# An eight-tap causal matrix convolution on one core: the first outputs as direct products, and one more block

## The chip, the cores and the metric

The kernel runs on one NeuronCore of one Trainium2 chip. Five engines run their own queues in order and meet only at semaphores: TensorE (PE, matrix multiply into PSUM), VectorE (DVE), ScalarE (ACT), GpSimd (POOL) and SyncE (SP). POOL and SP here mostly issue DMAs: POOL those that also convert fp32 to bf16, SP the stores of the output and the DMA transposes. The metric is the device time in microseconds (us), as a median of runs; lower is better.

## What is computed

`x` has 8 sequences of 4096 steps of 512 features, `kernel` has 8 taps of 512 x 512, and each output is a sum over the eight most recent steps:

```python
for k in range(K):              # K = 8
    shifted = x if k == 0 else concat([zeros(B, k, D), x[:, :-k, :]], axis=1)
    out += matmul(shifted, kernel[k])
```

The steps before a sequence's start count as zero. Inputs and outputs are fp32; the kernel multiplies in bf16 and sums in fp32.

## The kernel before, in words

**Tiling.** All 32768 steps are cut into 128 runs of RUN = 256 steps, one run to a partition. "Row t" is step t of all 128 runs at once, a tile of 128 x 512. Sixteen runs make a sequence, so the seven rows before row 0 are the last seven rows of the run before, moved by one partition, with zeros where a sequence begins. TensorE wants rows with the features on the partitions: `XR` is a ring of R = 20 transposed rows, and row t lies at `place(t) = (t + 4) % 20`.

**Products.** The unit of work is `product` (L116): one transposed row, or a sum of rows, times one 512 x 512 weight, as four matmuls of 128 x 128 by 128 x 512 that accumulate in one PSUM bank. Eight taps done directly would cost eight products per output. The kernel saves most of them by sums. A node (class at L122) computes four outputs with four taps' worth of combined weights. Its kinds are H1 (taps 4 to 7), H0 (taps 0 to 3), PL (their sum) and MI (their difference). Inside a node the four taps are split again in pairs (LO, HI, MID). A node that is not a leaf takes 9 products and a leaf takes 11. Four nodes, PL, MI, H1 and an H0 leaf, give a block of twelve outputs for 38 products, where 96 would be direct.

**What a node does.** `node_z` (L137) sums or subtracts seven rows of the ring into `Z`; `node_s` (L151), `node_A` (L148) and `node_F` (L154) sum those again into the operands; `node_a1`, `node_a0`, `node_u`, `node_v` and `node_l` are products; `node_seed` and `node_dts` are ACT copies between PSUM banks; `node_d` (L200) combines two banks on DVE; `node_e` (L233) takes the result out, and with `middle` (L261) joins it with the other nodes' results and stores it. A node's first product needs `node_A`, its products on `F` need `node_F` and `node_d`.

**Weights.** `load_w` (L266) loads one tap. All other weights are sums of taps, 128 x 2048 elements each: `wsum` (L270) and `plus` (L281) make them on DVE. Four of the PL weights and one of the MI weights are made without DVE: ACT copies or negates a tap (`seed_plus`, or the scalar multiplication at L393), and a DMA issued by POOL adds another tap to it (`add_h0`, L328).

**The head.** The first HEAD = 16 outputs are done in two groups of eight with six nodes: n0 (16 direct products, `direct` at L312, on sums of rows), n1 to n3 (leaves, 11 each) and n4 and n5 (9 each), 67 products in all. Outputs of n0 to n3 wait in SBUF, three of these eight tiles in space that PL weights take later (`held`, L79), until n4 and n5 are added to them by `node_y` (L226), and `store_first` stores them. Rows for the head are loaded into weight tiles not yet in use (`xin`, L287) and transposed on PE (`transpose_pe`, L296) against an identity; `fill` (L293) is two matmuls of zeros whose result nobody uses.

**The order.** The kernel states the order of every queue itself (`manual_schedule`, L49). The head, L331 to L562, is one long list of steps written out. After it NB = 20 blocks of STEP = 12 outputs run through `SLOT` (L563), a list of step names for each kind of node, in which each node's steps are mixed with the preparation of the next two. Loads of `x` go as fp32 to bf16 copies into DRAM (`load_x`) and from there through a DMA transpose on SP (`transpose_x`) into the ring, four rows at a time. PSUM is used as three pairs of banks for outputs and one pair (`pair(3)`) for a node's common terms; a pair is free for its next user when the last reader of its former content is done.

Of the kernel before, what the change touches and what calls it, by code (L numbers as in the profile page):

```python
# [8 lines left out]
LO, HI, MID = 0, 1, 2  # L9
H1, H0, MI, PL = 0, 1, 2, 3  # L10
LEAF = (1, 2, 3)
# [3 lines left out]
def kernel(  # L15
# [13 lines left out]
    HEAD, STEP, R = 2 * K, 12, 20  # L29
# [16 lines left out]
    dpool = ctx.enter_context(tc.tile_pool(name="xd", bufs=NB * STEP // 4, space=bass.MemoryType.DRAM))  # L46
# [6 lines left out]
    W = {}  # L53
# [23 lines left out]
    D4, D42, zero = WP[:, 0:8], Z[:, 0:8], Z[:, 10]  # L77
    E4, T4, T42 = W[MI, MID, HI], W[MI, MID, LO], W[MI, MID, MID]
    held = {(2, 1): WP[:, 8:12], (0, 0): WP[:, 12:16], (0, 1): WP[:, 16:20]}  # L79
# [42 lines left out]
    class Node:  # L122
        def __init__(self, k, t, a, comps=None):
            self.k, self.t, self.a, self.comps = k, t, a, comps
            self.z, self.o = (XR, place(t - 3)) if k < 6 else (Z, 4 if a in (MI, H0) else 0)
            self.leaf = k in LEAF or k >= 6 and a == H0
            self.p = {}
# [31 lines left out]
    def comps(n):  # L159
        s, a = SX[n.k % 2], AX[n.k % 2]  # L160
        u, s = n.comps or (n.z[:, n.o + 3], [s[:, j] for j in range(5)])
        return u, [a[:, 0], a[:, 1]], s, [F[:, j] for j in range(4)]
# [58 lines left out]
    first, cc, dd = {}, {}, {}  # L221
# [4 lines left out]
    def node_y(n, b_, a):  # L226
        y = first[n.t, a, b_]
        tt(y, y, n.p[b_], ADD if a == H1 else SUB)

    def store_first(t, a, b_):  # L230
        store(t + 4 * a + 2 * b_, first[t, a, b_])

    def node_e(n, b_):  # L233
        p, t = n.p[b_], n.t + 2 * b_
        if n.k < 4:
            y = wide(held[n.k, b_]) if (n.k, b_) in held else y_tile()
            nc.scalar.copy(out=y, in_=p)
            first[n.t, n.a, b_] = y
        elif n.k < 6:
            node_y(n, b_, H1)  # L240
            node_y(n, b_, H0)
        elif n.a == PL:
# [42 lines left out]
    H, HF = XR[:, 8:16], wide(WP[:, 0:8])  # L285
    XF = XR[:, 0:8]
    xin = {(0, 0): WP[:, 12:16], (0, 4): WP[:, 16:20], (8, 0): W[PL, LO, LO], (8, 4): W[PL, HI, LO]}  # L287

    def load_xin(t, h):
        rows(xin[t, h], t + h, 4)  # L290

    bank = {}
    def fill(pw):  # L293
        for h in range(2):
            nc.tensor.matmul(pw[:, h], lhsT=zero[:, 0:P], rhs=zero, start=True, stop=True)  # L295
    def transpose_pe(name, k, src, t0, t1):  # L296
        o = pair(k).bitcast(bf).rearrange("p a (b d) -> p (a b) d", b=2)
        for t in range(t0, t1):
            for c in range(DC):
                nc.tensor.transpose(o[:, t - t0, c * P:(c + 1) * P], src[:, t, c * P:(c + 1) * P],  # L300
                                    ident)
        bank[name] = o[:, 0:t1 - t0]
    nodes = [
        Node(0, 0, H1),
        Node(1, 8, H1, (T4[:, 0], [D42[:, 7]] + [T42[:, j] for j in range(4)])),
        Node(2, 0, H0, (D4[:, 4], [D42[:, j] for j in range(3, 8)])),
        Node(3, 8, H0, (D4[:, 4], [D42[:, j] for j in range(3, 8)])),
        Node(4, 0, MI), Node(5, 8, MI)]
    nodes += [Node(6 + 4 * k + i, HEAD + STEP * k, a) for k in range(NB)
              for i, a in enumerate((PL, MI, H1, H0))]  # L310
    n0, n1, n2, n3, n4, n5, n6, n7 = nodes[:8]
    def direct(m, t):  # L312
        n = K // 2 - 1 - m
        product(n0.p[t // 2][:, t % 2], D4[:, t - m] if t >= m else E4[:, 4 + t - m],
                W[H1, n >> 1, n & 1], m == 0)
    def to(z):
        return z.rearrange("p t (c m) -> p t c m", m=P)[:, :, :, 1:P]
    def prev(z):
        return z.rearrange("p t (c m) -> p t c m", m=P)[:, :, :, 0:P - 1]
    def first_run(z):  # L320
        nc.vector.memset(z[:, :, 0:D:G], 0.0)
    X4, X8 = XR[:, 8:12], XR[:, 12:16]
    def start_n0():
        n0.p = {0: pair(0), 1: pair(1)}
    def seed_plus(b_, c_):
        nc.scalar.copy(out=W[PL, b_, c_], in_=W[H1, b_, c_])

# [3 lines left out]
    start_n0()  # L331
    nc.vector.memset(zero, 0.0)
    for k in range(6):
        fill(pair(k % 4))
    load_xin(0, 0)
    fill(pair(2))
    make_identity(nc, ident)
    transpose_pe("x0", 2, xin[0, 0], 0, 2)
    load_xin(0, 4)
    rows(H[:, 1:4], RUN - 7, 3)  # L340
    nc.sync.dma_start(out=HF, in_=xr[:, RUN - 4:RUN, :])
    load_w(4)
    nc.scalar.copy(out=H[:, 4:6], in_=HF[:, 0:2])
    load_w(5)
    nc.scalar.copy(out=H[:, 6:8], in_=HF[:, 2:4])
    nc.scalar.copy(out=XF[:, 4:6], in_=bank["x0"])
    transpose_pe("h0", 3, H, 4, 6)
    nc.scalar.copy(out=to(XF[:, 0:2]), in_=prev(bank["h0"]))
    first_run(XF[:, 0:2])
    fill(pair(3))  # L350
    fill(pair(2))
    tt(D4[:, 0:2], XF[:, 0:2], XF[:, 4:6], ADD)
    transpose_pe("h1", 0, H, 6, 8)
    nc.scalar.copy(out=to(XF[:, 2:4]), in_=prev(bank["h1"]))
    first_run(XF[:, 2:4])
    fill(pair(3))
    fill(pair(3))
    load_xin(8, 0)
    transpose_pe("xb", 0, xin[0, 0], 2, 4)
    direct(0, 0)  # L360
    load_w(6)
    nc.vector.tensor_copy(out=XF[:, 6:8], in_=bank["xb"])
    tt(D4[:, 2:4], XF[:, 2:4], XF[:, 6:8], ADD)
    direct(0, 1)
    transpose_pe("he", 1, H, 1, 4)
    fill(pair(2))
    fill(pair(2))
    seed_plus(HI, HI)
    direct(0, 2)
    transpose_pe("x1", 2, xin[0, 4], 0, 4)  # L370
    tt(to(E4[:, 1:4]), prev(bank["he"]), to(XF[:, 1:4]), ADD)
    first_run(E4[:, 1:4])
    load_w(7)
    fill(pair(3))
    fill(pair(3))
    direct(1, 1)
    nc.vector.tensor_copy(out=X4, in_=bank["x1"])
    fill(pair(3))
    tt(D42[:, 3], D4[:, 1], D4[:, 3], ADD)
    transpose_pe("x2", 2, xin[8, 0], 0, 4)  # L380
    direct(1, 2)
    load_w(3)
    nc.scalar.copy(out=X8[:, 2:4], in_=bank["x2"][:, 2:4])
    tt(D4[:, 4:8], XF[:, 4:8], X4, ADD)
    tt(D42[:, 4:8], D4[:, 2:6], D4[:, 4:8], ADD)
    wsum(H1, MID, HI)
    wsum(H1, MID, LO)
    direct(2, 0)
    nc.scalar.copy(out=X8[:, 0:2], in_=bank["x2"][:, 0:2])
    tt(T4, X4, X8, ADD)  # L390
    direct(0, 3)
    direct(3, 1)
    nc.scalar.mul(out=W[MI, HI, LO], in_=W[H1, HI, LO], mul=-1.0)  # L393
    fill(pair(3))
    direct(3, 0)
    direct(3, 2)
    direct(2, 1)
    wsum(H1, MID, MID)
    tt(AX[1][:, 0], D4[:, 7], T4[:, 0], ADD)
    fill(pair(2))  # L400
    tt(T42[:, 2:4], T4[:, 0:2], T4[:, 2:4], ADD)
    direct(3, 3)
    load_w(1)
    wsum(H0, MID, LO)
    load_w(0)
    load_w(2)
    tt(AX[1][:, 1], T4[:, 0], T4[:, 1], ADD)
    wsum(MI, HI, HI)
    node_a1(n1)
    tt(T42[:, 0:2], D4[:, 6:8], T4[:, 0:2], ADD)  # L410
    direct(2, 2)
    direct(1, 3)
    node_a0(n1)
    node_u(n1)
    node_seed(n1, 0)
    direct(2, 3)
    direct(1, 0)
    wsum(H0, MID, HI)
    wsum(H0, MID, MID)
    load_xin(8, 4)  # L420
    load_x(16)
    node_l(n1, 0, LO)
    tt(AX[0], D4[:, 3:5], D4[:, 4:6], ADD)
    node_e(n0, 0)
    node_seed(n1, 1)
    node_l(n1, 0, HI)
    node_s(n5)
    wsum(MI, LO, HI)
    wsum(MI, MID, HI)
    nc.scalar.copy(out=D4[:, 2:4], in_=T4[:, 2:4])  # L430
    add_h0(MI, HI, LO)
    node_s(n4)
    node_l(n1, 1, HI)
    node_a1(n2)
    wsum(MI, LO, LO)
    node_e(n0, 1)
    node_a0(n2)
    node_e(n1, 0)
    transpose(12, xin[8, 4])
    wsum(MI, LO, MID)  # L440
    tt(D4[:, 4:8], X8, XR[:, 16:20], ADD)
    node_u(n2)
    node_seed(n2, 0)
    seed_plus(LO, HI)
    node_A(n4)
    node_l(n1, 1, LO)
    node_l(n2, 0, LO)
    nc.scalar.copy(out=D42[:, 3], in_=T42[:, 3])
    add_h0(PL, LO, HI)
    node_l(n2, 0, HI)  # L450
    node_seed(n2, 1)
    node_a1(n3)
    node_l(n2, 1, LO)
    tt(AX[1], D4[:, 3:5], D4[:, 4:6], ADD)
    node_u(n3)
    node_a0(n3)
    wsum(MI, MID, LO)
    behind(AX[1][:, 0])
    load_x(36)
    node_e(n1, 1)  # L460
    node_l(n2, 1, HI)
    node_e(n2, 0)
    node_seed(n3, 1)
    node_seed(n3, 0)
    wsum(MI, MID, MID)
    node_a1(n4)
    transpose_x(16)
    tt(D42[:, 4:8], D4[:, 2:6], D4[:, 4:8], ADD)
    node_l(n3, 0, LO)
    node_F(n4, 1)  # L470
    node_l(n3, 0, HI)
    plus((MID, LO))
    node_e(n2, 1)
    plus((MID, HI))
    node_e(n3, 0)
    load_x(20)
# [160 lines left out]
```

## Time and profile before

| what | value |
|---|---|
| median of three runs | 758.33 us (757.30 to 759.14) |
| the profiled execution | 759.11 us, its span 757.3 us |
| PE, DVE, ACT, POOL busy in the span | 733.1, 690.1, 254.9, 62.0 us |
| weight loads on PE from `product` | 3308 (827 products of four) |
| first matmul of a `product` begins | 15.61 us |
| last PE work in the chain of waits ends | 752.8 us |

"Busy" for PE includes fills and transposes. Matmul records can be missing, so products are counted by the weight loads, of which none is. In the page's slices PE is busy to nine tenths or more from the seventh slice of 18.9 us on, up to the last one, and falls below that in slices 1, 5 and 6. DVE is busy to nine tenths from the sixth slice on, up to the last.

### The profile page before, as it was taken

What the parts mean: (1) busy time and instruction counts of PE and PEld (TensorE: products, weight loads), DVE (VectorE), ACT (ScalarE), POOL (GpSimd) and SP (SyncE); (2) the same over time, 40 slices, a digit from 0 to 9 for tenths busy, and PEclk for the clock granted to TensorE, in tenths of its full rate; (3) what the DMA queues carried; (4) which work ended last, traced back from release to release, by engine and by line L of the source; (5) the groups of instructions that cost most, each with busy time, mean ns of one, the idle gap of its engine ahead of it and who ended that gap; (6) DMA issues with size and microseconds to landing.
All of it is one profiled execution on the core that took longest, in us unless ns stands there. A gap on an engine that the chain in (4) does not pass through costs nothing.

```text
span 757.3 us, 8900 instructions
## 1 busy us (share of the span) xinstructions
PE 733.1 (97%) x3352; PEld 331.8 (44%) x3420; DVE 690.1 (91%) x727; ACT 254.9 (34%) x380; POOL 62.0 (8%) x103
## 2 busy tenths in 40 slices
PE   6999689999999999999999999999999999999997
PEld 2544234444444444444444444444444444444443
DVE  1774899999999999999999999999999999999996
ACT  4264332333333233333323333332423323232331
POOL 5020201010010101101010110101011010100000
PEclk9999899999999999999999999999999999999999
DMA  9979797976959688796968869796786969775424
GB/s 206 207 140 162 195 255 173 211 200 161 245 136 237 162 195 215 149 238 148 243 160 180 241 140 236 146 238 168 185 234 136 242 145 224 184 178 169 136 84 167
DMA packets 159948, 141.51 MB, mean 187 GB/s; under 512 B 130208, under 2 KB 134304, under 8 KB 159776
## 3 DMA queue, kind: packets, MB, share of 16 engines
q1 hardware_dynamic: 145456, 99.89, 48.6%
q0 software_dynamic: 14304, 40.77, 29.6%
q8 instruction: 27, 0.44, 0.2%
q10 hardware_dynamic: 144, 0.26, 0.1%
q14 instruction: 17, 0.14, 0.1%
HBM read 77.33 MB, written 98.57 MB: 232 GB/s over the span
## 4 chain that ended last, share of the span: by engine, by line
PE 91%; DMA 4%; DVE 2%; issue 1%; ACT 0%; POOL 0%; DVEq 0%; ACTq 0%; POOLq 0%
PE pp L118 91%; DMA w<-in_kernel_dram 2%; DMA out_dram<-w 1%; DMA XR<-xd 1%; DVE y L82 1%; DVE w L82 1%; PE pp L295 0%; DVE S L82 0%; PE pp L300 0%; ACT pp L188 0%; DVE Z L82 0%; DVE F L82 0%; ACT pp L169 0%; ACT pp L190 0%; DVE pp L82 0%
## 5 line engine op out<-in xcount | busy, mean ns | idle before, releaser
L118 PE MATMUL pp<-w,S 128*128 128x512 bf16 x1114 | 261.6, 381 | 5.7 <-ACT pp L190 3.9
L118 PE MATMUL pp<-w,F 128*128 128x512 bf16 x973 | 245.3, 379 | 2.9 <-DVE pp L82 1.7
L118 PE MATMUL pp<-w,A 128*128 128x512 bf16 x668 | 173.2, 380 | 3.1 <-ACT pp L169 0.7
L118 PEld LDWEIGHTS <-S 128*128 128x128 bf16 x1136 | 111.2, 98 | 140.7 <-issue 9.5
L82 DVE TENSOR_TENSOR Z<-XR 128x3584 bf16<-128x3584 bf16 (+2 forms) x104 | 146.9, 1430 | 4.1 <-DMA XR<-xd 4.1
L118 PEld LDWEIGHTS <-F 128*128 128x128 bf16 x992 | 97.0, 98 | 119.5 <-issue 2.3
L82 DVE TENSOR_TENSOR S<-Z 128x2560 bf16<-128x2560 bf16 x80 | 118.4, 1480 | 0.0
L188 ACT COPY pp<-pp 128x1024 f32<-128x1024 f32 (+1 forms) x85 | 58.7, 691 | 157.5 <-PE pp L118 152.7
L118 PEld LDWEIGHTS <-A 128*128 128x128 bf16 x680 | 66.2, 98 | 85.7 <-issue 5.2
L172 ACT COPY pp<-pp 128x512 f32<-128x512 f32 x62 | 35.3, 570 | 201.2 <-PE pp L118 201.2
L118 PE MATMUL pp<-w,Z 128*128 128x512 bf16 x378 | 96.8, 379 | 1.0 <-DVE w L82 0.5
L82 DVE TENSOR_TENSOR F<-S 128x1024 bf16<-128x1024 bf16 x124 | 84.5, 682 | 0.0
L107 POOL COPY junk<-A 128x2 bf16<-128x2 bf16 x19 | 18.6, 978 | 540.3 <-DVE A L82 540.3
L190 ACT ACTIVATE pp<-pp 128x1024 f32<-128x1024 f32 (+1 forms) x85 | 59.6, 701 | 4.8 <-DVE y L82 3.8
L118 PEld LDWEIGHTS <-Z 128*128 128x128 bf16 x388 | 38.0, 98 | 46.4 <-issue 0.8
L207 DVE SCALAR_TENSOR_TENSOR pp<-pp,DT 128x512 f32<-128x512 f32 x62 | 42.9, 692 | 16.3 <-PE pp L118 15.6
L247 DVE SCALAR_TENSOR_TENSOR y<-pp,y 128x1024 f32<-128x1024 f32 x40 | 48.8, 1220 | 8.6 <-PE pp L118 8.1
L82 DVE TENSOR_TENSOR A<-Z 128x1024 bf16<-128x1024 bf16 x80 | 54.9, 686 | 1.3
L82 DVE TENSOR_TENSOR y<-y,pp 128x1024 f32<-128x1024 f32 (+1 forms) x46 | 54.3, 1187 | 1.9 <-PE pp L118 1.9
L244 ACT ACTIVATE y<-pp 128x1024 f32<-128x1024 f32 x40 | 41.1, 1027 | 42.2 <-PE pp L118 42.2
L82 DVE TENSOR_TENSOR y<-pp,y 128x1024 f32<-128x1024 f32 x40 | 48.6, 1216 | 1.7 <-DMA out_dram<-y 1.7
L262 DVE SCALAR_TENSOR_TENSOR y<-y 128x1024 f32<-128x1024 f32 x40 | 48.6, 1216 | 0.0
(53 smaller groups left out, 278.8 us busy)
## 6 DMA issues: line engine op xcount, KB each, us to landing
out_dram<-y SPq DMA_DIRECT2D x124, 512.0 KB, 7.7
xd<-in_x_dram POOLq DMA_DIRECT2D x60, 512.0 KB, 10.8
w<-in_kernel_dram POOLq DMA_DIRECT2D x8, 512.0 KB, 20.8
w<-w POOLq DMA_DIRECT2D x5, 512.0 KB, 6.8
w<-in_x_dram POOLq DMA_DIRECT2D x4, 512.0 KB, 11.7
out_dram<-w SPq DMA_DIRECT2D x3, 512.0 KB, 6.8
w<-in_x_dram SPq DMA_DIRECT2D x1, 1024.0 KB, 4.9
XR<-xd SPq DMA_TRANSPOSE x60, 5.4
```

The source lines that it names most:

```text
L82: nc.vector.tensor_tensor(out=o, in0=a, in1=b, op=op)
L107: nc.gpsimd.tensor_copy(out=junk, in_=z[:, 0:2])
L118: nc.tensor.matmul(bank, lhsT=comp[:, c * P:(c + 1) * P], rhs=w[:, c, :], start=start and c == 0, stop=c == DC - 1, skip_group_check=True)
L172: nc.scalar.copy(out=n.q[:, 0], in_=n.q[:, 1])
L188: nc.scalar.copy(out=o, in_=q)
L190: nc.scalar.mul(out=o, in_=q, mul=-1.0)
L207: nc.vector.scalar_tensor_tensor(out=p[:, 0], in0=p[:, 1], scalar=-1.0, in1=DT, op0=MUL, op1=SUB)
L244: nc.scalar.mul(out=cc[b_], in_=p, mul=0.5)
L247: nc.vector.scalar_tensor_tensor(out=dd[b_], in0=p, scalar=-0.5, in1=cc[b_], op0=MUL, op1=ADD)
L262: nc.vector.scalar_tensor_tensor(out=cc[b_], in0=cc[b_], scalar=2.0, in1=dd[b_], op0=MUL, op1=SUB)
```

## The change

The head's node tree goes. The first HEAD = 4 outputs are 4 x 8 direct products of a row and a tap (`direct(tap, t)`), and NB = 21 blocks follow from t = 4, all of PL, MI, H1 and H0 (leaf). The class loses what only the head's nodes used; `node_y`, `store_first`, `first`, `held`, the tiles D4, D42, E4, T4 and T42, and every call of `add_h0` and `seed_plus` go. All combined weights come from `wsum` and `plus` on DVE. The rows 0 to 3 are loaded by SP as fp32 into `XF` and cast by DVE and ACT; rows 4 to 7 and 8 to 11 come by POOL, the last ones in two loads of two rows. The steps of the first four nodes are also written out one by one, through `go(k, name)`, which runs the step of that name as `SLOT` would. In that list a call that has nothing to do (such as `go(3, "v1")`, whose next node is a leaf) emits nothing.

```diff
-LEAF = (1, 2, 3)
+LEAF = ()
...
-    HEAD, STEP, R = 2 * K, 12, 20
+    HEAD, STEP, R = K // 2, 12, 20
...
-    D4, D42, zero = WP[:, 0:8], Z[:, 0:8], Z[:, 10]
-    E4, T4, T42 = W[MI, MID, HI], W[MI, MID, LO], W[MI, MID, MID]
-    held = {(2, 1): WP[:, 8:12], (0, 0): WP[:, 12:16], (0, 1): WP[:, 16:20]}
+    H, zero = WP[:, 0:8], DT.bitcast(bf)[:, 0:D]
+    xin = {0: W[MI, MID, MID], 4: W[MI, MID, HI], 8: W[MI, MID, LO]}
...
-    def node_y(n, b_, a):
-        y = first[n.t, a, b_]
-        tt(y, y, n.p[b_], ADD if a == H1 else SUB)
...
+    def history(eng, t, name):
+        z = XR[:, place(t):place(t) + bank[name].shape[1]]
+        eng(out=to(z), in_=prev(bank[name]))
         nc.vector.memset(z[:, :, 0:D:G], 0.0)
+    def here(eng, t, name, a, b):
+        eng(out=XR[:, place(t) + a:place(t) + b], in_=bank[name][:, a:b])
+    def cast(eng, a, b):
+        eng(out=xin[0][:, a:b], in_=XF[:, a:b])
+    def direct(tap, t):
+        n = K - 1 - tap
+        product(pd[t // 2][:, t % 2], XR[:, place(t - tap)], W[n >> 2, n >> 1 & 1, n & 1], tap == 0)
+    def direct_out(b_):
+        y = y_tile()
+        nc.scalar.copy(out=y, in_=pd[b_])
+        store(2 * b_, y)
+    def z_rows(n, a, b):
+        zsum(a, n.t - 3 + a, n.t + 1 + a, b - a, ADD)
+    def s_rows(n, a, b):
+        tt(SX[n.k % 2][:, a:b], Z[:, a:b], Z[:, a + 2:b + 2], ADD)
...
+    pd = {0: pair(0), 1: pair(1)}
+    load_w(0)
+    rows(H[:, 4:8], RUN - 4, 4)
+    make_identity(nc, ident)
+    nc.vector.memset(zero, 0.0)
+    nc.sync.dma_start(out=XF, in_=xr[:, 0:4, :])
+    cast(nc.vector.tensor_copy, 2, 4)
+    for k in range(7):
+        fill(pair(2 + k % 2))
+    cast(nc.scalar.copy, 0, 2)
+    transpose_pe("x0", 2, xin[0], 0, 4)
+    load_w(4)
+    here(nc.scalar.copy, 0, "x0", 2, 4)
+    load_w(5)
+    load_w(1)
+    here(nc.scalar.copy, 0, "x0", 0, 2)
+    load_w(7)
+    direct(0, 3)
+    direct(0, 2)
+    transpose_pe("h4", 3, H, 4, 8)
+    history(nc.scalar.copy, -4, "h4")
+    load_w(3)
+    plus((HI, HI))
+    wsum(H1, HI, MID)
...
+    load_w(6)
+    direct(1, 0)
+    rows(H[:, 1:4], RUN - 7, 3)
...
+    load_w(2)
+    load_xin(4)
...
+    load_xin(8, 0, 2)
...
+    transpose_pe("x8", 2, xin[8], 0, 2)
+    here(nc.scalar.copy, 4, "x4", 0, 2)
+    here(nc.scalar.copy, 4, "x4", 2, 4)
+    fill(pair(3))
+    transpose_pe("x9", 2, xin[8], 2, 4)
+    direct(7, 1)
+    direct(6, 1)
+    wsum(MI, LO, HI)
+    direct(5, 0)
+    wsum(PL, LO, MID)
+    direct(6, 0)
+    load_x(12)
+    here(nc.scalar.copy, 8, "x8", 0, 2)
+    wsum(MI, MID, HI)
+    wsum(PL, MID, MID)
+    wsum(MI, LO, MID)
+    z_rows(nodes[1], 0, 5)
+    load_x(16)
+    node_A(nodes[1])
+    here(nc.scalar.copy, 10, "x9", 0, 2)
+    z_rows(nodes[1], 5, 7)
+    direct_out(0)
+    node_a1(nodes[1])
+    load_x(20)
+    load_x(24)
+    s_rows(nodes[1], 0, 3)
+    direct(2, 3)
+    node_u(nodes[1])
...
+    s_rows(nodes[1], 3, 5)
+    transpose_x(12)
+    node_z(nodes[2])
+    node_A(nodes[2])
+    node_F(nodes[1], 0)
...
+    for k in range(5, len(nodes)):
+        for name in SLOT[nodes[k].a].split():
+            go(k, name)
```

## The prediction

> **What bounds the kernel now.** I first split the span into stages by windows, for the instructions of `product` alone. Columns: stage, its length, PE busy (records), weight loads busy (records), granted clock, DMA share, GB/s. Four weight loads are one product.
>
> ```profile
> 0.00:15.50 15.50, 0.00 (x0) 0.00 (x0) 1.00 0.95 205
> 15.50:46.00 30.50, 24.59 (x101) 10.49 (x105) 0.94 1.16 202
> 46.00:77.00 31.00, 29.58 (x134) 13.27 (x136) 1.00 0.75 136
> 77.00:103.40 26.40, 18.06 (x66) 7.11 (x67) 0.87 0.90 218
> 103.40:757.30 653.90, 646.16 (x2940) 292.58 (x3000) 1.00 0.76 187
> ```
>
> From 103.4 to 430 us the trace has 1510 weight loads in 326.6 us: 216.3 ns each, **0.865 us a product**, with no room between them. So from 103.4 us on PE is the bound, and nothing there can be gained except by fewer products. Before that, 77 products (308 loads) are worth 66.6 us and take 103.4. **Lost: 36.8 us**, by stage: 15.5 with no product, then 30.5 - 26.25 x 0.865 = 7.8 (row transposes, fills, clock), 31.0 - 34 x 0.865 = 1.6, and 26.4 - 16.75 x 0.865 = 11.9. After the last product 4.4 us pass to the end of the span.
>
> Next, what made the fourth stage lose 11.9 us, by the timeline (start, duration, instruction, in brackets the idle time before it and who ended it):
>
> ```profile
> 75.43 1.23 DVE L82 TENSOR_TENSOR Z<-XR 128x2048 bf16<-128x2048 bf16 x1 [4.06 <-DMA XR<-xd]
> 81.77 3.57 PE L118 MATMUL pp<-w,S 128*128 128x512 bf16 x8 [3.86 <-ACT pp L190]
> 91.44 1.23 DVE L82 TENSOR_TENSOR w<-w,w 128x2048 bf16<-128x2048 bf16 x1 [1.99 <-DMA out_dram<-w]
> 99.70 1.02 PE L118 MATMUL pp<-w,F 128*128 128x512 bf16 x3 [1.72 <-DVE pp L82]
> ```
>
> DVE waits for transposed rows, then runs behind: PE waits for an ACT seed that itself waited for `node_y` on DVE. Eight matmuls then start 446 ns apart. At 91 us a weight sum waits until an output held in weight space is stored. DVE is busy 24.4 of these 26.4 us (all-engine windows).
>
> **The price of the change in PE work.** Before, 67 + 20 x 38 = 827 products; after, 32 + 21 x 38 = 830: **+2.6 us**. Transposes stay 76, fills go from 18 to 13. The tail keeps its steps, 4.4 us. All else is how much is lost in the new head, so I lay it out queue by queue.
>
> **Loads (POOL).** Its timeline before:
>
> ```profile
> 8.41 0.74 POOL L88 DMA_DIRECT2D w<-in_kernel_dram  x1 [1.29 <-DMA w<-in_x_dram]
> 10.85 0.74 POOL L88 DMA_DIRECT2D w<-in_kernel_dram  x1 [1.70 <-DMA w<-in_x_dram]
> 12.71 0.74 POOL L88 DMA_DIRECT2D w<-in_kernel_dram  x1 [1.12 <-DMA XR<-in_x_dram]
> 15.75 0.74 POOL L88 DMA_DIRECT2D w<-in_kernel_dram  x1 [2.30 <-DMA w<-in_kernel_dram]
> 18.25 0.54 POOL L88 DMA_DIRECT2D w<-in_x_dram  x1 [1.76 <-DMA w<-in_kernel_dram]
> 20.71 0.56 POOL L88 DMA_DIRECT2D xd<-in_x_dram  x1 [1.92 <-DMA w<-in_x_dram]
> ```
>
> The ninth to fourteenth load each wait for the landing of the first to sixth, in order of issue. So these starts are landings: 2.4 us for four rows, 1.9 for three, 3.0 and 2.5 for a weight, 2.5 for four rows. I take 2.65 a weight and 0.63 a row; this puts the last weight of before at 36.7, and DVE's wait for a weight indeed ends at 36.79. **A rule speaks against the change here**: the Trainium skill (DMA: Bandwidth & Descriptors, "Anatomy of one DMA") has a DMA cost about 2.0 us fixed plus bytes over 436 GB/s, so smaller parts pay the fixed part again. A weight (1.05 MB) would be 4.4 us and halving the load of rows 8 to 11 would add 2.0. The row says 2.5 to 3.0 and 1.9 for the smaller piece: with eight loads in flight the fixed part lies under the others. I take the row. The rule, read as a serial price, is the third rival.
>
> The first load lands near 8.4 again (the SP load of 1 MB runs beside it, as before). Then, in the new order: rows -4..-1 at 10.9, tap 4 at 13.6, tap 5 16.2, tap 1 18.9, tap 7 21.5, tap 3 24.2, tap 6 26.8, rows -7..-5 28.7, tap 2 31.3, rows 4..7 33.8, rows 8,9 35.1, rows 10,11 36.3, rows 12.. 38.8. The last weight comes 5.4 us earlier than before because two tiles of rows moved behind it. None of these issues waits for an engine.
>
> **PE in the head.** Fills from 1.2 to 7.2 (fourteen at 427 ns, the spacing of the first ones before). Rows 0..3 land at 5.7 (SP load before); the casts take 1.0 on ACT (`CAST` row) and between 0.69 (DVE COPY of 1024) and 1.04 on DVE, both under the fills: nothing. Sixteen transposes 1.1, ACT copy 1.0: first product at **9.5 instead of 15.6**. Then I follow the listed order with 0.865 a product against the landings. `history` of four rows is not in the trace: 1.0 (half of it) to 2.0 (two halves); I take 1.9, and `direct(4, 3)` starts at 14.9. `direct(4, 1)` ends 18.8, `(1, 0)` waits for tap 1 until 18.9; `(7, 3)` ends 24.9, `(3, 0)` 28.3, the second history's transposes 30.9, `(2, 2)` 32.6, `(7, 0)` 37.1. The transposes of rows 10,11 use the PSUM pair of rows 8,9, so PE waits for that copy, 38.1 to 38.8, and behind it stand the last four products. They end at **42.9**; 31 products are done, 16.1 us lost. No gap exceeds 1 us.
>
> **DVE in the head.** Sums run back to back at 1.13 us start to start:
>
> ```profile
> 26.72 2.35 DVE L82 TENSOR_TENSOR w<-w,w 128x2048 bf16<-128x2048 bf16 x2
> L82 DVE TENSOR_TENSOR S<-Z 128x2560 bf16<-128x2560 bf16 x80 | 118.4, 1480 | 0.0
> L82 DVE TENSOR_TENSOR Z<-XR 128x3584 bf16<-128x3584 bf16 x36 | 72.5, 2014 | 0.0
> ```
>
> There were 21 on DVE, now 26: +5.7 us, while five ACT copies of 1.9 and five accumulating DMAs go. Starting at 15.0 (tap 4, then behind the history's memset), the first 22 end at 40.5. They wait for a landing only at taps 5 and 1. Rows 8,9 are copied by 38.8, so `z_rows(0, 5)` runs to 41.9, `node_A` to 42.5, `z_rows(5, 7)` to 43.1, the two parts of `s` to 44.6. Splitting costs little: 1.40 + 0.60 against 1.93 start to start for z, nothing that matters for s. What it buys is that `node_A` need not wait for rows 10,11 (copied 40.5), 0.6 us. With `A` at 42.5, PE goes straight on at 43.3 after a fill: no stall at the first node.
>
> **The first block.** Both engines, step by step: PE finishes node 1's `v1` at 48.5, `a1` of node 2 at 49.4 (its `A` 47.1), `l00` 50.2 (its `d` 48.3), `a0` 52.0 (weight sum MID, LO done 50.6), `u` 52.8 (51.8), `v0` 55.4 (S at 53.2), `a1` of node 3 57.1 (A at 56.3), `v1` of node 3 63.1. Then `a1` of node 4 waits for the last sum (MID, MID) until **64.1**: 1.0 stall. At 64.1, 54 products are done: 64.1 - 46.7 = **17.4 lost**. DVE has hardly a gap from 15 to 78 us here, against 96.6% in the steady stage (315.4 of 326.6), where it has about 1.1 us a block free. So whatever DVE is late, PE loses once, and it isn't soon made up.
>
> **What I can't walk.** Rows 16 to 27 come by transposes that SP issues behind the two stores of the direct outputs and when the ring's old rows are read: about 56 and 63 us, needed by `node_z` of node 5 at 70.8. With 5.4 us a transpose (DMA issues) and 512 KB stores ahead (7.7), that is close; the second block's `z` is queued on DVE ahead of everything that PE needs next. The bounds are 0 and 11.9, the loss of the corresponding stage before; I take **3.5**, near the 4.06 that DVE waited for rows there, as the second block has three sets of rows to come but few stores. The node additions (eight of 1.2 us), the held outputs and the adding DMAs, which made the rest of the 11.9, are gone.
>
> **The clock.** The Trainium skill (TensorE: Matmul & The Clock Gate, "The HAM clock gate") halves the clock after an idle window of some 3.4 us. In the trace 1.64 us idle before 15.61 sufficed for matmuls 427 ns apart until 18.9; 0.73 at 46.67 didn't. By the rule a 1.5 us stall in the first block is free, by the row it can add 1.7 (eight matmuls at 0.21). I count it within the 3.5.
>
> **The sum.** Loss 17.4 + 3.5 = 20.9 for 36.8, a gain of 15.9, less 2.6: **-13.3**. On the profiled execution: 757.3 - 13.3 = 744.0 of span, 745.8 with the 1.8 outside it (759.11). The median was 0.8 below this execution: **745.0**. With the unwalked term at its bounds: 741.5 to 753.4.
>
> **Rivals.**
> *A, the wait moves (747 to 756.8).* DVE has no slack: if weights land 3 us later, or each of some 60 operations takes 0.1 more, DVE is 5 to 6 us later at the first block; PE loses that and a cold stretch of 1.7, beside rows as late as before: 753. For it: 100% DVE and the wait at 75.43. Against it: sums overlap at 1.13 as observed.
> *B, as walked with nothing unwalked: 741.5.* For it: PE had no stall in any later block of before, and few stores run early.
> *C, loads bound the head: slower.* All the direct products and 22 sums need taps in the order of one queue. By the rule's serial price each weight is 1.75 and each four rows 1.9 later than by the row (three rows as much), so tap 2 lands 7 x 1.75 + 2 x 1.9 = 16.1 later, and rows 10,11, behind three more loads, about 22. The first node starts 16 to 22 later, and it turns slower from 13.3; at 18 the time is 763. Against it: six landings in the trace.
> *D, within 0.2%:* only if A's two losses and half of C's come together.
>
> **Chances.** Forecast (742 to 747, B's end included) 0.53, A 0.30, D 0.05, C 0.12. A measurement tells 0.2% (1.5 us) from no change. Faster 0.83, same 0.05, slower 0.12. The range, 740 to 757, leaves out C, D and a little below.
>
> **What would show it.** First product at 9.5; last direct product but one near 43; fewer than 22 us lost in the first 103 us; no PE idle over 2 us. A PE gap at 24 to 35 ended by a weight's landing speaks for C; DVE waiting for `XR<-xd` near 70, or PE for DVE between 60 and 90, for A. The forecast is wrong if the landings exceed 2.65 us or the steady stage has idle PE.

## The result, and the profile after

746.34 us (746.14 to 746.51, four runs) against 757.82 us for the kernel before in the same comparison: a ratio of 0.985, 95% interval 0.983 to 0.9865. The forecast was 745.0, with a range of 740 to 757. The span of the profiled execution went from 757.3 to 744.8 us. Over all comparisons, executions of the kernel before took 754.7 to 759.5 us, so the profiled one, at 759.1, lies near the top of its spread, and what profiles differ by is somewhat more than what medians differ by.

The windows of the kernel after, for `product` alone (L117 there; stage, length, PE busy, weight loads, clock, DMA share, GB/s):

```profile
0.00:15.50 15.50, 3.76 (x16) 1.56 (x18) 1.00 0.97 197
15.50:46.00 30.50, 25.72 (x113) 11.05 (x115) 1.00 1.15 211
46.00:77.00 31.00, 28.23 (x128) 12.57 (x130) 1.00 0.72 165
77.00:103.40 26.40, 25.58 (x117) 11.53 (x118) 1.00 0.91 211
103.40:744.80 641.40, 633.49 (x2884) 286.86 (x2940) 1.00 0.76 185
```

At 216.3 ns each, the 381 weight loads up to 103.4 us are worth 82.4 us: **21.0 lost, where it was 36.8**. By stage: 11.6 (15.5), 5.6 (7.8), 2.9 (1.6), 0.9 (11.9). The fourth stage gave 11.0 us and the start 3.9; twelve more weight loads cost 2.6. After 103.4 us, 5.5 us aren't products, against 5.0. Sum: 15.8 - 2.6 - 0.5 = 12.7; the spans differ by 12.5.

How the head runs, by PE's timeline (start, duration, instruction, idle time before it and who ended it):

```profile
9.48 1.90 PE L117 MATMUL pp<-w,XR 128*128 128x512 bf16 x8
40.07 0.61 PE L280 MATMUL pp<-ident,w 128*128 128x128 bf16 x8 [0.67 <-ACT XR L296]
44.40 1.03 PE L117 MATMUL pp<-w,A 128*128 128x512 bf16 x4
48.38 1.02 PE L117 MATMUL pp<-w,A 128*128 128x512 bf16 x4 [1.21 <-ACT pp L189]
55.31 1.02 PE L117 MATMUL pp<-w,Z 128*128 128x512 bf16 x4 [0.72 <-ACT DT L193]
63.91 1.02 PE L117 MATMUL pp<-w,Z 128*128 128x512 bf16 x4 [0.68 <-ACT DT L193]
82.05 1.02 PE L117 MATMUL pp<-w,A 128*128 128x512 bf16 x4 [0.70 <-ACT pp L187]
```

The first product begins at 9.48 us. Node 1 begins at 44.40 without a wait, and the four short waits from there to 82 us are all for ScalarE copies, none for VectorE or a DMA. `a0` of nodes 1 and 5 stands behind seed copies in the list, and `u` of nodes 2 and 3 behind a copy into `DT`, on the same pair of banks.

POOL's timeline, where the waits again end at landings (first to sixth, tenth and twelfth load):

```profile
9.40 0.55 POOL L87 DMA_DIRECT2D w<-in_x_dram  x1 [1.26 <-DMA w<-in_kernel_dram]
11.86 0.74 POOL L87 DMA_DIRECT2D w<-in_kernel_dram  x1 [1.91 <-DMA w<-in_x_dram]
14.45 0.54 POOL L87 DMA_DIRECT2D w<-in_x_dram  x1 [1.84 <-DMA w<-in_kernel_dram]
16.95 0.54 POOL L87 DMA_DIRECT2D w<-in_x_dram  x1 [1.96 <-DMA w<-in_kernel_dram]
19.49 0.53 POOL L87 DMA_DIRECT2D w<-in_x_dram  x1 [2.00 <-DMA w<-in_kernel_dram]
23.07 0.55 POOL L87 DMA_DIRECT2D xd<-in_x_dram  x1 [3.04 <-DMA w<-in_kernel_dram]
32.53 0.52 POOL L87 DMA_DIRECT2D xd<-in_x_dram  x1 [2.02 <-DMA w<-in_kernel_dram]
36.25 0.52 POOL L87 DMA_DIRECT2D xd<-in_x_dram  x1 [0.69 <-DMA w<-in_x_dram]
```

VectorE in the same time, by windows of all engines (busy time of PE, PEld, DVE, ACT, POOL):

```profile
15.50:43.00 27.50, 25.82 (x149) 12.85 (x151) 26.47 (x24) 5.38 (x5) 4.74 (x9) 1.00 1.16 210
43.00:65.00 22.00, 19.33 (x89) 8.47 (x88) 21.03 (x24) 9.50 (x14) 0.00 (x0) 1.00 0.99 213
65.00:80.00 15.00, 14.89 (x69) 6.84 (x70) 14.96 (x16) 4.15 (x6) 1.72 (x4) 1.00 0.40 94
```

VectorE is busy 96% from 15.5 to 43, 96% to 65 and 99.7% to 80 us. PE loses 2.7 of the 22 us in the middle and nearly nothing from 65 on. ScalarE, in contrast, is busy for only 5.4 of the 27.5 us up to 43.

### The profile page after: what moved, and what is told of

It is laid out like the page before. It is cut to its first block, busy times and chain, and to the rows that moved or that the text cites. A ratio compares the mean times of both kernels' runs of the same rounds, so it can differ in the third digit from the quotient of the medians.

```text
span 744.8 us, 8881 instructions
## 1 busy us (share of the span) xinstructions
PE 729.3 (98%) x3354; PEld 331.0 (44%) x3422; DVE 697.2 (94%) x729; ACT 241.3 (32%) x369; POOL 57.8 (8%) x98
## 4 chain that ended last, share of the span: by engine, by line
PE 93%; ACT 1%; issue 1%; DVE 1%; DVEq 0%; ACTq 0%
PE pp L117 92%; ACT pp L187 0%; DVE w L81 0%; PE pp L280 0%; ACT DT L193 0%; ACT XR L296 0%; DVE pp L81 0%; DVE pp L206 0%; DVE y L81 0%; ACT pp L189 0%; DVEq L625 0%; ACT pp L168 0%; ACT pp L171 0%; PE pp L274 0%; DVE F L81 0%
## 5 line engine op out<-in xcount | busy, mean ns | idle before, releaser
L117 PE MATMUL pp<-w,S 128*128 128x512 bf16 x1153 | 269.0, 379 | 1.5
L117 PE MATMUL pp<-w,F 128*128 128x512 bf16 x986 | 248.4, 379 | 1.0
L117 PEld LDWEIGHTS <-S 128*128 128x128 bf16 x1176 | 114.8, 98 | 140.2 <-issue 3.6
L117 PE MATMUL pp<-w,A 128*128 128x512 bf16 x659 | 170.5, 379 | 2.7 <-ACT pp L189 1.2
L81 DVE TENSOR_TENSOR Z<-XR 128x2048 bf16<-128x2048 bf16 (+3 forms) x109 | 154.6, 1437 | 0.1
L117 PEld LDWEIGHTS <-F 128*128 128x128 bf16 x1008 | 98.6, 98 | 119.0
L81 DVE TENSOR_TENSOR S<-Z 128x2560 bf16<-128x2560 bf16 (+1 forms) x85 | 124.8, 1469 | 0.0
L187 ACT COPY pp<-pp 128x512 f32<-128x512 f32 x84 | 57.3, 682 | 158.8 <-PE pp L117 154.0
L117 PEld LDWEIGHTS <-A 128*128 128x128 bf16 x672 | 65.2, 97 | 82.8 <-DVE A L81 4.5
L171 ACT COPY pp<-pp 128x512 f32<-128x512 f32 x63 | 35.9, 570 | 198.9 <-PE pp L117 198.9
L117 PE MATMUL pp<-w,Z 128*128 128x512 bf16 x330 | 85.4, 379 | 1.7 <-ACT DT L193 1.4
L189 ACT ACTIVATE pp<-pp 128x512 f32<-128x512 f32 x84 | 58.1, 692 | 1.1 <-PE pp L117 1.1
L206 DVE SCALAR_TENSOR_TENSOR pp<-pp,DT 128x512 f32<-128x512 f32 x63 | 43.9, 697 | 14.5 <-PE pp L117 14.5
L81 DVE TENSOR_TENSOR y<-y,pp 128x1024 f32<-128x1024 f32 (+1 forms) x43 | 51.1, 1190 | 2.0 <-PE pp L117 1.9
L117 PEld LDWEIGHTS <-Z 128*128 128x128 bf16 x336 | 32.9, 98 | 41.4 <-issue 1.5
## 6 DMA issues: line engine op xcount, KB each, us to landing
xd<-in_x_dram POOLq DMA_DIRECT2D x61, 512.0 KB, 10.8
w<-in_kernel_dram POOLq DMA_DIRECT2D x8, 512.0 KB, 15.9
```

Source lines behind the costliest of these rows:

```text
L81: nc.vector.tensor_tensor(out=o, in0=a, in1=b, op=op)
L117: nc.tensor.matmul(bank, lhsT=comp[:, c * P:(c + 1) * P], rhs=w[:, c, :], start=start and c == 0, stop=c == DC - 1, skip_group_check=True)
L171: nc.scalar.copy(out=n.q[:, 0], in_=n.q[:, 1])
L187: nc.scalar.copy(out=o, in_=q)
L189: nc.scalar.mul(out=o, in_=q, mul=-1.0)
L206: nc.vector.scalar_tensor_tensor(out=p[:, 0], in0=p[:, 1], scalar=-1.0, in1=DT, op0=MUL, op1=SUB)
```

## The experiments

Two theories went into them. **T:** in the head and the first block PE follows the landing of the taps, then VectorE's queue; what VectorE is late, PE loses once. **R:** the waits for ScalarE seen above set the first block, and VectorE is only busy. For the kernel before: VectorE's queue lost the 11.9 us (T), or late rows and stores did (R).

The runs were made on several chips; the kernel before ran beside each of them (medians of 756.5 to 758.1 us), the kernel after again only beside the three runs on GpSimd sums, halved weights and the order of rows.

**The kernel after, once more,** beside those three:

> The kernel after, unchanged, beside the next three on the same chip. All theories: 746.3 us (746.1 to 746.5 so far), with single executions up to 1.5 us later where the first weight lands later or the clock rises later.

Measured: 746.45 us (746.04 to 747.33). One of its four runs is 0.8 above the rest.

**More work on VectorE.**

```diff
     wsum(MI, LO, MID)
+    for _ in range(3):
+        wsum(PL, LO, MID)
     z_rows(nodes[1], 0, 5)
```

> The kernel after, with one weight sum (PL; LO, MID) made three times more on VectorE just ahead of the first node's row sums: 3 x 1.13 = 3.4 us more work in VectorE's queue. Theory (VectorE has no slack in the head, and PE waits for it once): the whole delay reaches the end, 746.3 + 3.4 = 749.7 us, the first product of node 1 moves from 44.4 to about 47.3 us, and the product losses before 103 us grow by about as much. Rival (the waits for ScalarE's copies, not VectorE, set the first block): VectorE's delay is half absorbed, under 748 us. Rival (VectorE catches up within some blocks, and PE with it): nothing, 746.3.

Measured: 752.2 us (751.79 to 752.88), 5.8 more, for 3.4 us of work. Its PE timeline, at node 1's first product, and the window with the clock:

```profile
48.18 1.89 PE L117 MATMUL pp<-w,A 128*128 128x512 bf16 x4 [3.26 <-DVE A L81]
```

```profile
44.10:65.00 20.90, 15.70 (x64) 6.49 (x63) 18.44 (x20) 8.34 (x12) 0.00 (x0) 0.92 0.77 164
```

PE waits 3.26 us for `A`, and four matmuls then take 1.89 us in place of 1.03: the clock falls to 0.92 on average over 20.9 us, 1.7 us worth. Node 1 begins 3.8 us later than in the kernel after (48.18 for 44.40), and the cold stretch adds its 1.7, which makes up the difference of the spans (750.3 and 744.8). So the delay comes through whole, and the gap that it opens costs half as much again. Later nothing is caught up. T, and more than T said.

**Fewer waits for ScalarE.**

```diff
-    node_seed(nodes[1], 0)
-    node_seed(nodes[1], 1)
     node_a0(nodes[1])
+    node_seed(nodes[1], 0)
+    node_seed(nodes[1], 1)
     node_dts(nodes[1])
...
-    go(1, "dt")
     go(1, "u")
+    go(1, "dt")
```

(likewise for node 3; node 5's `a0` moves up behind its `u`).

> The kernel after, in which node 1's a0 product stands before the two seed copies, and the DT copies of nodes 2 and 3 stand behind the u product; node 5's a0 moves behind its u. Theory (four waits of PE for ScalarE in the first block, 1.21, 0.72, 0.68 and 0.70 us, come from the order of a copy and a product on the same pair of banks): three to four of these waits vanish, 746.3 - 2.5 = about 743.8 us. Rival (VectorE, busy without a gap, is what sets the block): PE waits for VectorE's row and weight sums instead, and the time stays within 0.7 us of 746.3.

Measured: 746.29 us (745.98 to 747.88): no gain in the median. The four waits did go, but shorter ones for VectorE (0.19 twice) and others for ScalarE (0.71 and 0.30 up to node 4) came in their place. The chain of waits of that kernel runs through VectorE from 51.9 to 68.6 us with pauses of at most 0.38; its last pieces, and PE's timeline:

```profile
63.82 1.39 DVE S L81
65.21 1.14 DVE y L232
66.35 1.13 DVE Z L81
67.48 1.15 DVE w L81
68.62 0.04 issue
68.67 14.85 PE pp L117 x68
```

```profile
10.56 3.07 PE L117 MATMUL pp<-w,XR 128*128 128x512 bf16 x8 [1.83 <-DMA w<-in_kernel_dram]
50.80 1.89 PE L117 MATMUL pp<-w,S 128*128 128x512 bf16 x8 [0.71 <-ACT pp L187]
60.94 1.04 PE L117 MATMUL pp<-w,A 128*128 128x512 bf16 x4 [0.19 <-DVE A L81]
68.67 1.02 PE L117 MATMUL pp<-w,Z 128*128 128x512 bf16 x4 [0.19 <-DVE w L81]
```

(This profiled execution began its direct products 1.1 us late and cold, and its node 1 at 46.46, 2.1 us behind the one above.) In the kernel after, VectorE ended the last weight sum at 67.06 and PE took it up at 67.37: the two were level within 0.3 us.

```profile
50.37 0.69 DVE L81 TENSOR_TENSOR pp<-DT,pp 128x512 f32<-128x512 f32 x1 [0.80 <-PE pp L117]
65.84 1.22 DVE L81 TENSOR_TENSOR w<-w,w 128x2048 bf16<-128x2048 bf16 x1
67.37 1.03 PE L117 MATMUL pp<-w,Z 128*128 128x512 bf16 x4
```

So R fails in the main: most of the waits for ScalarE were worth nothing by themselves. Not quite all: from node 1 to node 4 PE took 22.97 us in the kernel after and 22.21 here, 0.76 of the 2.6 us of waits. The median shows none of it; as the kernel after did not run on that chip, the worth is only known to lie between nothing and about 0.8.

**Rows not divided.**

```diff
-    load_xin(8, 0, 2)
+    load_xin(8)
...
-    load_xin(8, 2, 4)
...
-    z_rows(nodes[1], 0, 5)
+    z_rows(nodes[1], 0, 7)
```

(transposes, copies and `s_rows` undivided in the same way).

> The kernel after, with rows 8 to 11 loaded, transposed, copied and summed undivided (one load of four rows, one copy of 2048, one row sum of seven rows, one of five). By the prediction's working, node 1's A waits for rows 10 and 11 and for a sum of seven rows instead of five: about 0.6 us on VectorE and up to 1.5 on PE, where the wait of 0.67 us for the pair of banks goes away: 746.5 to 748. By the rule that each load pays about 2.0 us anew, the undivided form saves it: 744.5 to 745.5.

Measured: 748.37 us (748.0 to 748.67): dividing is worth about 1.9 us, somewhat more than the working had. PE's timeline:

```profile
45.21 1.04 PE L117 MATMUL pp<-w,A 128*128 128x512 bf16 x4 [0.97 <-DVE A L81]
```

Node 1 now waits 0.97 us for VectorE and begins 0.8 later than in the kernel after. The rest isn't placed: the profiled execution's first weight landed 1.0 us later than the other's, though its last one did not. The smaller loads in any case cost nothing.

**Smaller loads everywhere.**

```diff
-        load(W[n >> 2, n >> 1 & 1, n & 1], kr[:, :, tap, :])
+        for c in (0, 2):
+            load(W[n >> 2, n >> 1 & 1, n & 1][:, c:c + 2], kr[:, c:c + 2, tap, :])
```

> The kernel after, with each of the eight weights loaded by two DMAs of half the size. By the landings in the trace (pace set by bytes, the fixed part hidden by the loads in flight): the landings stay within 1 us and the time within 1 us of 746.3. By the rule of about 2.0 us fixed for each DMA, paid one after the other: the last weight lands 8 x 2.0 = 16 us later and the time is near 746.3 + 14 = 760.

Measured: 745.86 us (745.5 to 746.25), 0.6 less than the kernel after beside it, though the two ranges overlap. POOL's timeline:

```profile
12.47 0.71 POOL L87 DMA_DIRECT2D w<-in_kernel_dram  x1 [0.61 <-DMA w<-in_kernel_dram]
13.71 0.71 POOL L87 DMA_DIRECT2D w<-in_kernel_dram  x1 [0.53 <-DMA w<-in_kernel_dram]
14.99 0.71 POOL L87 DMA_DIRECT2D w<-in_kernel_dram  x1 [0.57 <-DMA w<-in_kernel_dram]
```

A half takes 1.24 to 1.28 us from landing to landing, half of a whole one. The fixed 2.0 us that the Trainium skill gives a DMA (DMA: Bandwidth & Descriptors, "Anatomy of one DMA") is not paid in series with eight in flight. What part of a load's latency it makes, these runs don't show: a half took a median of 10.3 us from issue to landing, a whole one 15.9.

**Rows ahead of the last weights.**

```diff
+    load_xin(4)
+    load_xin(8, 0, 2)
+    load_xin(8, 2, 4)
     load_w(6)
```

(and gone from behind them).

> The kernel after, with rows 4 to 11 loaded before taps 6 and 2 instead of behind them (as the kernel before had two tiles of rows ahead of its last weights). Taps 6 and 2 land 8 x 0.63 = 5.0 us later. Theory (PE and VectorE follow the landing of the taps): the sums and products that need taps 6 and 2 wait, the head ends 3 to 5 us later, with a cold stretch of up to 1.7 us: 749.5 to 753. Rival (VectorE's 22 sums, not the landings, set the head): under 1.5 us, below 748.

Measured: 751.18 us (749.95 to 751.64), 4.7 more. PE's timeline at the first product of tap 6:

```profile
32.67 3.33 PE L117 MATMUL pp<-w,XR 128*128 128x512 bf16 x8 [3.82 <-DMA w<-in_kernel_dram]
```

A wait of 3.82 us for the tap, then eight matmuls in 3.33 us. The order of the loads is worth this much.

**No first fills.** The line `fill(pair(2 + k % 2))` and its loop go.

> The kernel after, without its first seven fills (fourteen matmuls of zeros up to 7.2 us). By the trace of before (matmuls 427 ns apart for some 3.3 us after an idle time) the transposes and the first products run cold: 8 to 12 matmuls at 0.21 us more, so PE is 1.7 to 2.5 us later until 15 us, where it waits for the history in any case; part is absorbed there: 747 to 748.5. If the clock doesn't matter here: 746.4 or less.

Measured: 747.5 us (747.15 to 748.1), 1.1 more. PE's timeline:

```profile
6.56 1.89 PE L280 MATMUL pp<-ident,w 128*128 128x128 bf16 x16 [6.56 <-ACT w L304]
8.24 2.13 PE L274 MATMUL pp<-DT 128*128 128x512 bf16 x4
10.58 2.72 PE L117 MATMUL pp<-w,XR 128*128 128x512 bf16 x8 [0.21 <-DMA w<-in_kernel_dram]
```

Sixteen transposes take 1.89 us for 1.05, and eight matmuls 2.72 for 1.90. So the fills keep the clock up, and without them 0.8 us are lost twice. But how much of the 1.1 this makes is not shown: the first weight of this execution also landed 1.4 us later (at 10.8 for 9.4), and the first of the two losses lies ahead of that landing.

**The kernel before, part by part.** First without its node additions:

```diff
     def node_y(n, b_, a):
-        y = first[n.t, a, b_]
-        tt(y, y, n.p[b_], ADD if a == H1 else SUB)
+        pass
```

> The kernel before, with the additions of nodes 4 and 5 to the held outputs left out (eight VectorE additions of 1.2 us; the outputs 0 to 15 lack that part). Theory (VectorE's queue is what loses 11.9 us from 77 to 103 us): about 8 x 1.13 = 9 us come off VectorE's queue there and the loss shrinks by 6 to 9 us: 749 to 752 us. Rival (transposed rows and the stores that hold weight space set that stage): the loss shrinks by less than 3 us, 755 us or more.

Measured: 754.82 us (751.78 to 756.0) against 758.0: 3.2 less, between the two theories. From 77 to 103.4 us its profile has 92 weight loads, a loss of 6.5 us for 11.9. Its chain of waits shows what is next, and PE's timeline the wait at its end:

```profile
80.70 1.91 ACT w L325
82.61 0.28 issue
82.90 4.39 DMA w<-w
87.29 0.04 issue
87.33 1.04 PE pp L118 x4
```

```profile
87.33 1.02 PE L118 MATMUL pp<-w,Z 128*128 128x512 bf16 x4 [1.99 <-DVE w L82]
```

A sum made by a ScalarE copy (1.91 us) and an adding DMA (4.39): work taken off VectorE, but a chain of 6.6 us on the path. So I took it away too, with the sums on VectorE where the DMA stood:

```diff
-    seed_plus(HI, HI)
...
-    add_h0(PL, HI, HI)
+    plus((HI, HI))
```

(likewise for the other four).

> The kernel before, with the node additions left out as in the earlier run of it (the outputs 0 to 15 lack the part of nodes 4 and 5), and with its five sums by ScalarE copy and adding DMA made on VectorE at the place of the DMA. Theory (what is left of the loss from 77 to 103 us is the chain copy 1.9 us, adding DMA 4.4 us, next sum): five sums of 1.13 us join VectorE's queue, the chain goes, and the loss of that stage falls from 6.5 to under 4 us: 750 to 752.5, against 754.8 with the chain. Rival (VectorE's queue alone): 5.7 us more on VectorE, 757 or more.

Measured: 750.76 us (750.67 to 751.93) against 757.71. Its window for `product`, and VectorE's row sums that had waited for transposed rows:

```profile
77.00:103.40 26.40, 24.56 (x112) 10.72 (x111) 1.00 0.83 179
```

```profile
69.07 2.09 DVE L82 TENSOR_TENSOR Z<-XR 128x1536 bf16<-128x1536 bf16 x2
```

2.4 us lost. So of the 11.9 us some 5.4 went with the additions, 4.1 with the copies and adding DMAs, though VectorE got five more sums, and 2.4 stay. That is by the profiles; by the medians the additions are worth 3.2 and both together 7.0 us. Part of the difference is clock: in this stage it was 0.87 before (3.4 us worth), 0.94 without the additions and 1.00 here. VectorE's wait for transposed rows, 4.06 us before, was still 3.96 without the additions; here it is gone. So it came with the copies and adding DMAs.

**Two sums on GpSimd.**

```diff
-    wsum(H0, MID, HI)
-    wsum(H0, MID, MID)
+    pool_sub(W[H0, MID, HI], W[H0, HI, HI], W[H0, LO, HI])
+    pool_sub(W[H0, MID, MID], W[H0, MID, LO], W[H0, MID, HI])
```

(`pool_sub` is a subtraction on GpSimd, behind `load_x(32)`.)

> The kernel after, with the two weight sums that the first block needs last (H0; MID, HI and MID, MID) made by GpSimd from about 37 us on instead of VectorE: 2 x 1.13 = 2.3 us less in VectorE's queue between 59 and 67 us. Theory (VectorE and the waits for ScalarE's copies are level at the fourth node, within 0.3 us): the waits for the copies still stand, so 0.3 to 0.8 us are gained, 745.5 to 746. Rival (VectorE alone is the bound): 2.3 us gained, 744. Rival (GpSimd's sum and VectorE's operations slow each other, or GpSimd's sums take over 15 us each): same or slower, 746.3 to 749.

Measured: 757.33 us (756.4 to 758.01), 10.9 more. The timelines of POOL and VectorE:

```profile
35.02 9.08 POOL L271 TENSOR_TENSOR w<-w,w 128x2048 bf16<-128x2048 bf16 x2
34.75 5.43 DVE L81 TENSOR_TENSOR w<-w 128x2048 bf16<-128x2048 bf16 x1
40.10 5.08 DVE L81 TENSOR_TENSOR w<-w,w 128x2048 bf16<-128x2048 bf16 x1
```

Two VectorE sums of 1.2 us took 5.4 and 5.1 while GpSimd made its two. VectorE lost about 8 us just ahead of node 1; PE waited 7.69 us there and lost clock as well. Node 1 began 7.5 us later than in the kernel after, and node 4 another 1.7. No theory had it so dear.

**VectorE and ScalarE relieved together.** The first try put four edits together: products ahead of the copies, weights in halves, and two sums made by copy and adding DMA.

```diff
+    seed_minus(LO, HI)
...
+    nc.scalar.mul(out=W[H0, MID, HI], in_=W[H0, LO, HI], mul=-1.0)
...
     load_x(12)
+    add_h0(MI, LO, HI)
+    nc.gpsimd.dma_start(out=W[H0, MID, HI], in_=W[H0, HI, HI], accum_op=ADD)
```

> The kernel after with four edits together: the products ahead of the ScalarE copies as in the earlier run, the weights in halves, and two weight sums taken off VectorE (MI; LO, HI and H0; MID, HI) by a negating ScalarE copy in its idle time before 37 us and an adding DMA behind the load of rows 12 to 15. Theory (VectorE's queue and PE's waits for ScalarE are level, so only both together bring something): 2 x 1.13 + 0.3 from the block and 0.5 from the first landing, 743.2 to 744.3. Rival (the adding DMAs delay the rows or the sums behind them): 745.5 or more.

Measured: 749.54 us (748.65 to 749.81), 3.1 worse than after. VectorE's timeline:

```profile
42.39 1.23 DVE L81 TENSOR_TENSOR w<-w,w 128x2048 bf16<-128x2048 bf16 x1 [4.43 <-DMA w<-w]
```

I had overlooked that the sum MI; MID, HI, ahead of node 1 in VectorE's queue, needs MI; LO, HI: VectorE stood 4.43 us for the adding DMA, which landed 9.3 us after its issue. The second try moved only H0; MID, HI:

> The kernel after with three edits: the products ahead of the ScalarE copies, the weights in halves, and only H0; MID, HI made by ScalarE copy and adding DMA (the sum MI; LO, HI stays on VectorE, as the sum MI; MID, HI right behind it needs it, which stopped VectorE for 4.4 us in the run before). Theory (VectorE's queue and PE's waits are level in the first block; only both together bring something): 1.13 off VectorE's queue with nothing waiting for it before 60 us, 0.3 to the tie, 0.5 from the first landing: 744 to 745. Rival (the adding DMA delays rows 16 to 27 and so the second block): 746 or more.

Measured: 745.08 us (744.62 to 745.3), just above the expected. That is below every run of the kernel after, and its span, 743.3 us, below 744.8 and 744.6. But the halved weights alone had a span of 743.7, and beside this run the kernel before took 756.51 us, so that the ratio, 0.9843 (0.9814 to 0.9872), does not differ from the 0.9846 of the kernel after. It has the lowest time that was measured; that it is faster than the halved weights, the times don't show. The traces show where each gained. PE's timeline at nodes 1 and 4:

```profile
44.43 1.03 PE L117 MATMUL pp<-w,A 128*128 128x512 bf16 x4
66.28 1.03 PE L117 MATMUL pp<-w,Z 128*128 128x512 bf16 x4
```

From node 1 to node 4 that is 21.85 us, for 22.97 in the kernel after and also with the halved weights alone, which began node 1 1.05 us earlier (43.35), and 22.21 with the products ahead of the copies. So here the first block itself became 1.1 us shorter: 0.8 with the order of the products and 0.4 more with the sum taken off VectorE, by one profiled execution of each. What the sum gives without the new order was not tried in a clean way, as GpSimd slowed VectorE down.

## Why the prediction was right, step by step

**The bound and the price of products** held: from 103.4 to 430 us both kernels have 1510 weight loads, so the steady stage runs at the same 216.3 ns, and the three products more are worth 2.6 us.

**The sum** said 20.9 us lost up to 103.4 us; 21.0 were. That is luck in part; it is closer than its parts deserve:

- **Loads.** The landings came at 9.4, 11.9, 14.5, 17.0, and the last weight at 32.5, where I had 8.4, 10.9, 13.6, 16.2 and 31.3: the spacing nearly right, the first landing a microsecond late. One landing, the sixth, took 3.6 us, over the 2.65 that I had named as a sign of being wrong; without the first fills it took 2.6 there, so it is no steady pace. Between the executions of the experiments the first landing varied from under 9 to 10.8 us. The serial price (rival C) is refuted by these landings, and by the halved weights.
- **PE in the head.** First product 9.48 (9.5). The last direct product ahead of node 1 ended at 44.0 (42.9), later by the landings.
- **VectorE in the head.** Sums done at 41.9 (40.5), `A` at 44.1 (42.5), and no wait of PE at node 1, as said.
- **The first block.** Here the working failed. It had PE reach node 4's `a1` at 64.1, after a stall of 1.0 us for the last weight sum. It did at 67.37, without that stall. On PE's side, of the 3.3, 1.1 came with the head; the waits of 1.21, 0.72 and 0.68 us for ScalarE add 2.6, the stall that didn't come takes 1.0 off, and 0.6 is spread over small gaps. I hadn't seen those waits: I let a product and a copy on the two banks of one pair run side by side. But VectorE would have held PE in any case: it ended the last weight sum at 67.06, 3.0 late. Of that, 1.6 came with the head and 0.6 is spread; only 0.8, its idle time at 50.37 for a product behind PE's first wait, comes from the waits. That is why removing them gave so little.
- **What couldn't be walked.** I took 3.5 us for late transposed rows. They cost nothing: no wait for rows shows there, and between 65 and 80 us PE is busy 14.89 of 15.00. The 4.06 us that I took as the model went with the copies and adding DMAs, which the change removes too. The 3.5 was right in size only, because the misses above cost 3.3 up to node 4. The mechanism that I named for it is wrong, and the agreement of the sum is luck.
- **The clock.** I read from the kernel before that 1.64 us of idle time suffice for half the clock. No wait of PE in the kernel after exceeds 1.21 us from its first fill on, so the reading wasn't put to work, but it does not hold as a rule: in the same trace 1.72 us idle at 99.70 were followed by matmuls at full clock, and so were 1.99 us without the additions. Ahead of the 1.64, PE had been busy for only 4.6 of the 9.5 us from 6 to 15.5, which may be what made the difference; that was not tried.

**Of the fourth stage of before** I said that the node additions, held outputs and adding DMAs were the rest of its loss. Shown by the profiles: the additions (5.4) and the copies with their adding DMAs (4.1, the late rows among them). The held outputs' share was not tried by itself.

**The last microsecond.** The span came out 0.8 above the forecast, half of it after 103.4 us. And I had put the median 0.8 below the profiled execution, as in the runs shown of the kernel before; for the kernel after it lies only 0.2 below (746.34 and 746.51). With 0.1 less outside the span than assumed, that is the 1.3 between 745.0 and 746.34.

**Rival A** did not come about, but was no illusion: three more sums on VectorE cost 5.8 us, cold stretch included, half of the gain. **B** (nothing unwalked, 741.5) was right that nearly nothing is lost behind node 4, and missed the 3.3 us ahead of it.

## What to carry to other kernels

Where two engines are level, a wait that the profile shows on one of them may be worth little alone: before removing it, look when the other engine delivers what the same instructions need next. In a start-up that is fed by one queue, order the loads by when each is needed and move nothing ahead of the last weights; smaller loads cost nothing here, with eight of them in flight. An operation handed to an idle engine by a copy and a DMA frees a queue and makes a chain, so ask how soon the result is needed, and list every reader.

## What the runs showed of the hardware

- GpSimd's subtraction of two 128 x 2048 bf16 operands took 4.5 us, and VectorE's sums beside it went from 1.2 to over 5 us.
- A delay can cost more than itself: after an idle 3.26 or 3.82 us, PE's next matmuls ran at about half clock, four in 1.89 us or eight in 3.33. Between 1.6 and 2.0 us the traces show both: eight matmuls in 3.07 us after an idle 1.83 (products ahead of copies, at 10.56), but full clock after 1.72 in the kernel before and 1.99 in the one without its additions.
- An adding DMA of 128 x 2048 bf16 took 4.39 us from issue to landing in the run without additions, and 9.3 us behind row loads in the first try of relieving both engines.
